# A decoder layer with product-key experts: the order of the v groups, the last u blocks kept on chip, and gathered rows dealt anew

## The chip, the cores and the metric

The kernel runs on one core of a Trainium2 chip. Its time is the device time in microseconds (us) of one execution; a verdict compares the medians of executions of two kernels. The engines are TensorE (PE: matmuls, with PEld for its weight loads), VectorE (DVE), ScalarE (ACT), GpSimd (POOL) and SyncE (SP). ScalarE, GpSimd and SyncE also issue DMA transfers; the sixteen DMA engines of the core carry all of them. Each engine runs its own instructions in the order in which they were written, and waits for others by semaphores.

## The reference

One layer of a hybrid decoder is run for 512 prompt tokens and 64 sample tokens (8 sequences of 8), with width D = 2048. Nearly all of the change lies in its last part, PEER, a layer of 16384 single-neuron experts of which each token uses 8 x 16:

```python
q = (xb @ w_q).reshape(PEER_BLOCK, PEER_HEADS, 2, HALF_DIM)
sc = jnp.einsum('thpk,pnk->thpn', q, sub_keys).astype(jnp.float32)
v1, i1 = lax.top_k(sc[:, :, 0], PEER_TOPK)
v2, i2 = lax.top_k(sc[:, :, 1], PEER_TOPK)
...
g = jax.nn.softmax(top, axis=-1).astype(xb.dtype)
act = jax.nn.gelu(jnp.einsum('td,thkd->thk', xb, expert_u[eidx])) * g
return jnp.einsum('thk,thkd->td', act, expert_v[eidx])
```

An expert's index is i1 * 128 + i2. Before PEER stand a modulated norm, a projection, a gated recurrence and a short convolution with an output projection; after it a residual and the final norm. Everything is in float32.

## The kernel before

**Two ways to the experts.** The kernel ranks the 128 values of i1 by how often they are picked. The experts of the first L = 84 of them (blocks of 128 experts) are computed densely for all 512 prompt tokens on TensorE; picks in the other 44 blocks, and all picks of the 64 samples, are computed sparsely: for each of 128 partitions (a token, or half the picks of a token) one row of `u` or `v` per column of a list is gathered from memory by an indirect DMA from GpSimd, 128 rows of 2048 numbers at once. Such a gather is called a row here. VectorE takes the dot product of a u row with the tokens' `hT` (L1230), or adds a v row, times its weight, to a sum in PSUM (L1258). The rows come in groups: the samples with 64, and five groups of prompt tokens, sorted by how many picks they have left, with 34, 43, 33, 27 and 10 (`GT`). Entries past a token's last pick are out of bounds, and nothing is fetched for them, so the last rows of a group are thin. Each prompt group's u rows begin with one fetch of its tokens (`h2r`, L1211), copied into `hT` by ScalarE (L1217). In all there are NU = 216 u uses (211 rows, 5 copies) and 211 v rows; v goes through the groups in the order 0, 2, 1, 3, 5, 4 (`VO`).

**The u stage.** `NU2` = 168 halves: block i, half c. For each, `load` fetches the block's weights with the SP queue into `raw` (512 KB), ScalarE copies them to `xhi` rounded (L903), GpSimd makes the rest `xlo` (L904), and TensorE runs 24 matmuls (L1356): three products for each of 8 slices, so that float32 accuracy is kept with rounded operands. `ahead(n + 3, n + 2)` loads three halves ahead and splits two ahead. After a block's second half ScalarE applies gelu into a tile `act` (three buffers, L1359) and writes it to memory, `actd` (256 KB, L1360). Beside it the routing weights are built densely block by block and written to memory, `gd`.

**The v stage.** `GROUPS` puts the blocks in ten groups of 8 and one of 4; for each, four quarters q of the output's columns; for each of these, four blocks (SG) at a time. That makes M = 84 steps of four columns kq with 12 matmuls each (L1376). The four blocks of a step share the activations of one such group of four, `sg`. Group sg needs: `load_weights` (four loads of 256 KB from `gd` into `gsb`, one buffer, with 512 contiguous bytes each), `load_group` (1024 KB from `actd` into `actr`, one buffer), `weigh` (their product on VectorE, L1319), and `halve` in two parts, `ahi` on ScalarE (L1326) and `alo` on VectorE (L1330). Both loads are issued on ScalarE's queue. The results in PSUM are moved or added to `acc` (L1396 ScalarE, L1398 VectorE).

**The seam.** For the last 18 halves, from n = E0 = 150 on, the groups sg 0 and 1 (the first eight blocks) are prepared by the code after `u_half`: loads of sg 0 at E0 + 1 to E0 + 4, `weigh` at E0 + 6, `halve` at E0 + 7 and E0 + 8; loads of sg 1 at E0 + 7 to E0 + 10, `weigh` at E0 + 14, `halve` at E0 + 15 and E0 + 16. From sg 2 on, `jobs` holds a list by column, worked out from `hi_at`, the column of the `halve` before it (it starts at -4): for sg 2 loads in columns 0 to 3, `weigh` in 8, `halve` in 12 and 14; the loads of sg 3 begin at column 10.

**The rows' order.** `gather_to(k)` issues uses up to number k, and in front of each use fetches up to three (in v four) rows ahead into four (in v six) slots. In the u stage the rows are dealt first by the time that is left over, and from half R2 on (all rows sorted) evenly, so that EARLY_V = 24 v rows are used by the end; past E0 with 0.8 of the slope. In v they are dealt by `room` (what a column has left) over the costs `cost` of the rows: 1.25 for the samples' rows, 1 for others. The result of a group goes to memory with a scatter, `accd`; groups with 64 tokens need two.

Of the kernel before, what the change touches and what calls it, by code (L numbers as in the profile page):

```python
# [30 lines left out]
NA = NP  # L31
# [19 lines left out]
HEADS_COUNTED = 4  # L51
FULL_ROWS = 1.25
LAG = 3
PAIRS = 6
EARLY_V = 24
HB = 4
# [23 lines left out]
def build(ctx, tc, A, O, dbg=None):  # L80
# [776 lines left out]

    steps, uses_of = [], {}
    b0 = 0
    for gi, sz in enumerate(GROUPS):  # L860
# [18 lines left out]
    def load(n):  # L879
        if n >= len(stream):  # L880
            return
        s = stream[n]
        k = n % 3 if n < NU2 + 2 else (n - NU2 - 2) % 4
        pool, b = (ws, 2) if k < 2 else (wx, 1) if k == 2 else (pools["vx"], 1)
        raw = pool.tile([128, 8, 128], F32, name=f"raw{n}", tag="wraw", bufs=b)
        if s[0] == "U":
            nc.sync.dma_start(raw, A["ut"][bass.ds(block(s[1]), 1), s[2]].rearrange("o p k c -> p (o k) c"))
        else:
            _, i, q = s
            r2 = raw.rearrange("p (a k) c -> p a (k c)", a=2)  # L890
            for a in range(2):
                nc.sync.dma_start(r2[:, a, :], A["vq"][bass.ds(block(i + a), 1), q].rearrange("o p c -> p (o c)"))
        raws[n] = raw
# [410 lines left out]
    def load_group(sg):  # L1304

        acts[sg] = ep.tile([128, SG, NA], F32, name=f"actr{sg}", tag="actr", bufs=1)
        nc.scalar.dma_start(acts[sg], actd[SG * sg:SG * sg + SG].rearrange("i p t -> p i t"))

    def load_weights(sg, q):

        if q == 0:
            gsb[sg] = ep.tile([128, NCH, SG * TC], F32, name=f"gsb{sg}", tag="gsb", bufs=1)
        nc.scalar.dma_start(gsb[sg][:, 4 * q:4 * q + 4, :],
                            gd[4 * q:4 * q + 4, :, sg * SG:(sg + 1) * SG, :].rearrange("c p i t -> p c (i t)"))

    def weigh(sg):

        a = acts[sg].rearrange("p i (c t) -> p i c t", t=TC)
        V.tensor_tensor(a, a, gsb.pop(sg).rearrange("p c (i t) -> p i c t", t=TC), op=ALU.mult)  # L1319

    def halve(sg, part):
# [24 lines left out]
    def u_half(n, i, c):  # L1346
# [10 lines left out]
        if c == 1:  # L1357
            act = actp.tile([128, NA], F32, name=f"act{i}", tag="act")
            S.activation(act, pu, AF.Gelu_apprx_tanh)  # L1359
            nc.scalar.dma_start(actd[i], act)  # L1360

# [236 lines left out]
    for n in range(NU2):  # L1598
# [36 lines left out]
        if not even:  # L1635
            if since is None and ready[0]:
                since = n
            if since is not None and n == since + 1:
                fetch_to(RB - 1)
            if R1 is not None and n > R1 + 1 and gf[0] in h_fetch and gf[0] <= gu[0] + 1:  # L1640
                fetch_to(gf[0] + 1)
# [9 lines left out]
        else:  # L1651
            gather_to(G0 + (NU + EARLY_V - G0) * (n - R2 - 0.2 * max(0, n - E0)) / (0.8 * (NU2 - 1) + 0.2 * E0 - R2))
        if n == E0:
# [5 lines left out]
        u_half(n, i, c)  # L1659
        for sg, o, first in ((0, 1, 0), (1, 8, 1)):  # L1660
            if n - E0 == o + 1:
                load_group(sg)
            if 0 <= n - E0 - o + first < 4:
                load_weights(sg, n - E0 - o + first)
            if n - E0 == o + 5 + sg:
                weigh(sg)
            if n - E0 == o + 6 + sg:
                halve(sg, 0)
            if n - E0 == o + 7 + sg:
                halve(sg, 1)  # L1670
    hp_.close()
# [11 lines left out]
    jobs = {}  # L1683
    hi_at = -4
    for sg in range(2, L // SG):
# [12 lines left out]
    for m in range(last):  # L1698
        for kq in range(KD // VQ):
            room[m, kq] = PIECE / 2 - 0.75 * steps[m][4] - 0.38  # L1700
    tot, run_ = sum(room.values()), 0.0
    fb = finish_b()
    fplan = {(last + 1, 2), (last + 2, 3), (last + 3, 1), (last + 3, 3), (last + 4, 1), (last + 4, 3)}
    NT = len(uses)
    cost = [FULL_ROWS if j < NU + bound[0] else 1.0 for j in range(NV0, NT)]
    sums = [sum(cost[:j + 1]) for j in range(len(cost))]
# [190 lines left out]
```

## Time and profile before

| | before |
|---|---|
| median of 3 runs | 3260.12 us (3255.20 to 3267.94) |
| profiled execution | 3266.23 us, span 3264.3 us |
| PE busy | 3107.0 us (95%) |
| DVE busy | 2144.3 us (66%) |
| POOL busy | 1720.4 us (53%) |
| ACT busy | 1074.1 us (33%) |
| u stage, first to last matmul of L1356 | 1197.6 to 2260.5 us |
| v stage, first to last matmul of L1376 | 2264.8 to 3236.7 us |

A row of a profile names line, engine, operation and tiles (out<-in, buffer numbers left out); "x" is a count. Behind the bar stand the busy time and the mean duration of one in ns, and then the idle time of that engine just before these instructions and who ended it. A row of the timeline begins with the start and the duration in us, and gives in brackets the idle time before it. A wait for several semaphores is put down to the one that came last. "q" behind an engine is its queue of DMA issues; q0, q1 and q10 in the tables of DMA queues are the gathers of GpSimd, the transfers of SP and those of ACT.

### The profile page before, as it was taken

Reading aid. Unit: us, or ns where it says so; the run is one execution under the profiler, and the core shown is the slowest. Engines: PE = TensorE matmul, PEld = TensorE weight load, DVE = VectorE, ACT = ScalarE, POOL = GpSimd, SP = SyncE. Lnnn points to the kernel's source line nnn. Section 1 sums busy time; section 2 is a strip of 40 time slices with the busy share of each in tenths; the row PEclk is TensorE's granted clock in tenths of the full one; section 3 lists DMA queues with packets and bytes.
Section 4 is the critical chain, followed back from the end, with each engine's and each line's share of the span. In section 5 each row is a group of like instructions: output and inputs, shape, how many; then the busy total and the mean of one; then the engine's idle time right before and its main releaser. Section 6 shows DMA issues by size and latency. Waiting matters only on the chain.

```text
span 3264.3 us, 53659 instructions
## 1 busy us (share of the span) xinstructions
PE 3107.0 (95%) x20695; PEld 2634.3 (81%) x20695; DVE 2144.3 (66%) x3238; ACT 1074.1 (33%) x1672; POOL 1720.4 (53%) x985
## 2 busy tenths in 40 slices
PE   5999999999989999999999999997999999999997
PEld 2688889899979998887778888875788888788776
DVE  5455521243346898887988888856566888778745
ACT  3344311132232222222656666522322222222222
POOL 2233233344343336666666666655666777677642
PEclk8999999999989999999999999998999999999998
DMA  9734465523342127889879898998999988899954
GB/s 371 291 137 147 164 217 207 207 82 135 130 155 70 69 89 282 311 309 380 312 288 387 326 382 343 376 355 330 348 349 368 395 315 301 320 376 337 354 183 153
DMA packets 305109, 869.09 MB, mean 266 GB/s; under 512 B 37610, under 2 KB 81514, under 8 KB 256650
## 3 DMA queue, kind: packets, MB, share of 16 engines
q1 hardware_dynamic: 165216, 390.87, 33.1%
q0 software_dynamic: 62880, 386.64, 30.3%
q10 hardware_dynamic: 76752, 88.10, 7.8%
q8 instruction: 163, 2.67, 0.3%
q14 instruction: 98, 0.80, 0.1%
HBM read 865.21 MB, written 68.90 MB: 286 GB/s over the span
## 4 chain that ended last, share of the span: by engine, by line
PE 55%; DMA 8%; issue 3%; DVE 2%; POOL 2%; ACT 0%; SPq 0%; ACTq 0%; POOLq 0%; DVEq 0%
PE pv L1376 23%; PE pu L1356 23%; DMA gsb<-gd 3%; PE qb L138 3%; PE qa L138 3%; DMA raw<-vq 2%; PE gbank L1554 1%; PE gx L1554 1%; DMA u<-u,rows 1%; DMA actd<-act 1%; POOL xlo L904 1%; PE sc L740 0%; PE pv L1380 0%; DMA tok<-accd 0%; DVE acc L1760 0%
## 5 line engine op out<-in xcount | busy, mean ns | idle before, releaser
L904 POOL TENSOR_TENSOR xlo<-raw,xhi 128x1024 fp32r<-128x1024 f32 x336 | 827.5, 2473 | 483.2 <-ACT xhi L903 475.3
L903 ACT ACTIVATE xhi<-raw 128x1024 fp32r<-128x1024 f32 x336 | 355.3, 1061 | 884.4 <-PE pv L1376 406.9
L1230 DVE SCALAR_TENSOR_TENSOR u<-u,hT 128x2048 f32<-128x2048 f32 x211 | 478.1, 2283 | 144.6 <-DMA u<-u,rows 132.8
L1258 DVE SCALAR_TENSOR_TENSOR accB<-v,dots,accB 128x2048 f32<-128x2048 f32 x199 | 468.3, 2353 | 154.5 <-DMA v<-v,rows 151.8
L1356 PE MATMUL pu<-hhi,xhi 128*128 128x512 f32 x1344 | 533.1, 397 | 11.9 <-ACT xhi L903 11.2
L1376 PE MATMUL pv<-ahi,xlo 128*128 128x512 f32 x1344 | 526.5, 392 | 14.2 <-POOL xlo L904 14.2
L1376 PE MATMUL pv<-ahi,xhi 128*128 128x512 f32 x1344 | 528.7, 393 | 11.3 <-ACT acc L1396 7.4
L1356 PE MATMUL pu<-hhi,xlo 128*128 128x512 f32 x1344 | 524.7, 390 | 6.2 <-POOL xlo L904 6.2
L1376 PE MATMUL pv<-alo,xhi 128*128 128x512 f32 x1344 | 526.4, 392 | 0.0
L1356 PE MATMUL pu<-hlo,xhi 128*128 128x512 f32 x1344 | 525.0, 391 | 0.0
L1376 PEld LDWEIGHTS pv<-ahi,xlo 128*128 128x128 f32 x1344 | 254.1, 189 | 71.0 <-POOL xlo L904 18.1
L1356 PEld LDWEIGHTS pu<-hhi,xhi 128*128 128x128 f32 x1344 | 253.2, 188 | 72.1 <-ACT xhi L903 11.6
L1376 PEld LDWEIGHTS pv<-ahi,xhi 128*128 128x128 f32 x1344 | 254.2, 189 | 64.3 <-ACT acc L1396 7.8
L1356 PEld LDWEIGHTS pu<-hhi,xlo 128*128 128x128 f32 x1344 | 253.2, 188 | 61.1 <-POOL xlo L904 8.0
L1376 PEld LDWEIGHTS pv<-alo,xhi 128*128 128x128 f32 x1344 | 254.6, 189 | 52.4
L1356 PEld LDWEIGHTS pu<-hlo,xhi 128*128 128x128 f32 x1344 | 253.3, 188 | 50.1
L1202 POOL DMA_INDIRECT u<-u,rows x211 | 213.3, 1011 | 149.2 <-DVE u L1230 104.4
L1202 POOL DMA_INDIRECT v<-v,rows x211 | 235.7, 1117 | 88.6 <-issue 34.0
L1548 ACT ACTIVATE op<-op,it 128x128 f32<-128x128 f32 x512 | 155.4, 389 | 0.5 <-issue 0.3
L1398 DVE TENSOR_TENSOR acc<-acc,pv 128x512 f32<-128x512 f32 x144 | 96.0, 682 | 86.5 <-PE pv L1376 82.0
L127 POOL TENSOR_TENSOR wlo_q<-raw_q,whi_q 128x1024 fp32r<-128x1024 f32 x28 | 68.0, 2427 | 151.6 <-ACT whi_q L125 151.6
L188 PE MATMUL ada<-wa,cpad 128*32 128x512 f32 x768 | 106.8, 652 | 40.8 <-DMA wa<-w_ada 40.8
(482 smaller groups left out, 5505.2 us busy)
## 6 DMA issues: line engine op xcount, KB each, us to landing
wa<-w_ada SPq DMA_DIRECT2D x96, 1024.0 KB
raw<-ut SPq DMA_DIRECT2D x168, 512.0 KB
raw<-vq SPq DMA_DIRECT2D x336, 256.0 KB
actd<-act ACTq DMA_DIRECT2D x84, 256.0 KB
gd<-stg ACTq DMA_DIRECT2D x64, 336.0 KB
gsb<-gd ACTq DMA_DIRECT2D x84, 256.0 KB
actr<-actd ACTq DMA_DIRECT2D x21, 1024.0 KB
raw_o<-w_out SPq DMA_DIRECT2D x32, 512.0 KB
```

Of the source, the lines that this page charges most:

```text
L127: lo_engine(share).tensor_sub(lo, raw, r32(hi))
L138: PE.matmul(o, st, mv[pick](k), start=first, stop=last)
L188: PE.matmul(acc[32 * g:32 * g + 32, :], cpad[:, 4 * kq + g, :], w[:, g, :], start=kq == 0, stop=kq == 3)
L903: S.activation(hi, raw, AF.Copy)
L904: G.tensor_sub(lo, raw, r32(hi))
L1202: G.indirect_dma_start(out=out, out_offset=None, in_=src, in_offset=bass.IndirectOffsetOnAxis(ap=idx, axis=0), bounds_check=NE * 128 - 1, ...
L1230: V.scalar_tensor_tensor(r, r, 1.0, st["h"], op0=ALU.mult, op1=ALU.mult, accum_out=dots[i][:, j:j + 1])
L1258: V.scalar_tensor_tensor(st["a"], r, dots[i][:, j:j + 1], st["a"], op0=ALU.mult, op1=ALU.add)
L1356: PE.matmul(pu, st[:, kk, :], movA[mv](k), start=k == 0 and a == 0, stop=k == KD - 1 and a == 2)
L1376: PE.matmul(pv, st, mv, start=first and j == 0 and a == 0, stop=last and not end and j == SG - 1 and a == 2)
L1398: V.tensor_add(ak, ak, pv)
L1548: S.activation(ops[:, j0 + j, :], ops[:, j0 + j, :], AF.Copy, scale=it[2][:, b * 4 + j:b * 4 + j + 1])
```

## The change

Six things are changed. (1) The v stage takes the groups of four in another order: first the blocks 0 to 3, then the last four, 80 to 83, then the others (`real`). (2) The gelu results of blocks 80 to 83 are not written to memory and read back: they stay in their `act` tiles, and `weigh_kept` multiplies each by its part of `gsb` straight into `actr`, two in half 166, one in half 167 and the last in column 0 of v; the two parts of `halve` follow in columns 1 and 2. (3) With that `hi_at` starts at 0: for the third group loads in columns 0, 1, 2 and 4, the activations in 5, `weigh` in 12, `halve` in 16 and 18; the weights of the fourth begin at column 14. (4) EARLY_V is 16 in place of 24, and past E0 the rows are dealt with 0.5 of the slope (EASE). (5) In v the room of the first four steps counts 0.7, the samples' rows cost 1, and a row of another group costs 0.35 plus 0.65 times a factor that falls from 1 towards 0 over the last 30% of its group. (6) In the u stage the fetch of a group's tokens may go out when two rows are still to be used, where it was one.

```diff
@@ -49,10 +49,10 @@
 RATE = (1.0, 1.7)
 PIECE_G = 6.3
 HEADS_COUNTED = 4
-FULL_ROWS = 1.25
 LAG = 3
 PAIRS = 6
-EARLY_V = 24
+EARLY_V = 16
+EASE = 0.5
 HB = 4
 SB = 10
 TK = 16
@@ -856,6 +856,12 @@
 
 
     steps, uses_of = [], {}
+    first_sg = [0, L // SG - 1]
+    real_sg = first_sg + [g for g in range(L // SG) if g not in first_sg]
+
+    def real(i):
+        return SG * real_sg[i // SG] + i % SG
+
     b0 = 0
     for gi, sz in enumerate(GROUPS):
         for q in range(VQ):
@@ -889,7 +895,7 @@
             _, i, q = s
             r2 = raw.rearrange("p (a k) c -> p a (k c)", a=2)
             for a in range(2):
-                nc.sync.dma_start(r2[:, a, :], A["vq"][bass.ds(block(i + a), 1), q].rearrange("o p c -> p (o c)"))
+                nc.sync.dma_start(r2[:, a, :], A["vq"][bass.ds(block(real(i) + a), 1), q].rearrange("o p c -> p (o c)"))
         raws[n] = raw
 
     def conv(n):
@@ -1304,19 +1310,30 @@
     def load_group(sg):
 
         acts[sg] = ep.tile([128, SG, NA], F32, name=f"actr{sg}", tag="actr", bufs=1)
-        nc.scalar.dma_start(acts[sg], actd[SG * sg:SG * sg + SG].rearrange("i p t -> p i t"))
+        nc.scalar.dma_start(acts[sg], actd[real(SG * sg):real(SG * sg) + SG].rearrange("i p t -> p i t"))
 
     def load_weights(sg, q):
 
         if q == 0:
             gsb[sg] = ep.tile([128, NCH, SG * TC], F32, name=f"gsb{sg}", tag="gsb", bufs=1)
         nc.scalar.dma_start(gsb[sg][:, 4 * q:4 * q + 4, :],
-                            gd[4 * q:4 * q + 4, :, sg * SG:(sg + 1) * SG, :].rearrange("c p i t -> p c (i t)"))
+                            gd[4 * q:4 * q + 4, :, real(SG * sg):real(SG * sg) + SG, :].rearrange("c p i t -> p c (i t)"))
 
     def weigh(sg):
 
         a = acts[sg].rearrange("p i (c t) -> p i c t", t=TC)
         V.tensor_tensor(a, a, gsb.pop(sg).rearrange("p c (i t) -> p i c t", t=TC), op=ALU.mult)
+
+    kept = []
+
+    def weigh_kept(j):
+
+        if j == 0:
+            acts[1] = ep.tile([128, SG, NA], F32, name="actr1", tag="actr", bufs=1)
+        g = gsb[1] if j < SG - 1 else gsb.pop(1)
+        V.tensor_tensor(acts[1][:, j, :].rearrange("p (c t) -> p c t", t=TC),
+                        kept.pop(0).rearrange("p (c t) -> p c t", t=TC),
+                        g[:, :, j * TC:(j + 1) * TC], op=ALU.mult)
 
     def halve(sg, part):
 
@@ -1357,7 +1374,10 @@
         if c == 1:
             act = actp.tile([128, NA], F32, name=f"act{i}", tag="act")
             S.activation(act, pu, AF.Gelu_apprx_tanh)
-            nc.scalar.dma_start(actd[i], act)
+            if i < L - SG:
+                nc.scalar.dma_start(actd[i], act)
+            else:
+                kept.append(act)
 
     pvs = {}
 
@@ -1637,7 +1657,7 @@
                 since = n
             if since is not None and n == since + 1:
                 fetch_to(RB - 1)
-            if R1 is not None and n > R1 + 1 and gf[0] in h_fetch and gf[0] <= gu[0] + 1:
+            if R1 is not None and n > R1 + 1 and gf[0] in h_fetch and gf[0] <= gu[0] + 2:
                 fetch_to(gf[0] + 1)
             if since is not None and n > since + 2:
                 due_g += RATE[R1 is not None] + (0.7 if waits and spare > 4.5 else 0.0)
@@ -1649,7 +1669,7 @@
                 spare = min(spare, 3.0)
             G0 = gu[0]
         else:
-            gather_to(G0 + (NU + EARLY_V - G0) * (n - R2 - 0.2 * max(0, n - E0)) / (0.8 * (NU2 - 1) + 0.2 * E0 - R2))
+            gather_to(G0 + (NU + EARLY_V - G0) * (n - R2 - (1 - EASE) * max(0, n - E0)) / (EASE * (NU2 - 1) + (1 - EASE) * E0 - R2))
         if n == E0:
             assert not pair and not stg
             put(len(puts))
@@ -1657,17 +1677,22 @@
             epx = ctx.enter_context(ExitStack())
             ep = epx.enter_context(tc.tile_pool(name="ep", bufs=1))
         u_half(n, i, c)
-        for sg, o, first in ((0, 1, 0), (1, 8, 1)):
-            if n - E0 == o + 1:
-                load_group(sg)
-            if 0 <= n - E0 - o + first < 4:
-                load_weights(sg, n - E0 - o + first)
-            if n - E0 == o + 5 + sg:
-                weigh(sg)
-            if n - E0 == o + 6 + sg:
-                halve(sg, 0)
-            if n - E0 == o + 7 + sg:
-                halve(sg, 1)
+        if n - E0 == 2:
+            load_group(0)
+        for sg, o in ((0, 1), (1, 7)):
+            if 0 <= n - E0 - o < 4:
+                load_weights(sg, n - E0 - o)
+        if n - E0 == 6:
+            weigh(0)
+        if n - E0 == 7:
+            halve(0, 0)
+        if n - E0 == 8:
+            halve(0, 1)
+        if n == NU2 - 2:
+            weigh_kept(0)
+            weigh_kept(1)
+        if n == NU2 - 1:
+            weigh_kept(2)
     hp_.close()
     vp = ctx.enter_context(tc.tile_pool(name="vp", bufs=1, side="right"))
     acc = vp.tile([128, KD, NA], F32, name="acc")
@@ -1681,7 +1706,10 @@
     last = M - VQ - ENDS
     KQ = KD // VQ
     jobs = {}
-    hi_at = -4
+    hi_at = 0
+    jobs[0] = [lambda: weigh_kept(3)]
+    jobs[1] = [lambda: halve(1, 0)]
+    jobs[2] = [lambda: halve(1, 1)]
     for sg in range(2, L // SG):
         use = uses_of[sg * SG]
         free = KQ * (uses_of[(sg - 3) * SG][-1] + 1) if sg >= 3 else 0
@@ -1697,12 +1725,16 @@
     room = {}
     for m in range(last):
         for kq in range(KD // VQ):
-            room[m, kq] = PIECE / 2 - 0.75 * steps[m][4] - 0.38
+            room[m, kq] = (PIECE / 2 - 0.75 * steps[m][4] - 0.38) * (0.7 if m < 4 else 1.0)
     tot, run_ = sum(room.values()), 0.0
     fb = finish_b()
     fplan = {(last + 1, 2), (last + 2, 3), (last + 3, 1), (last + 3, 3), (last + 4, 1), (last + 4, 3)}
     NT = len(uses)
-    cost = [FULL_ROWS if j < NU + bound[0] else 1.0 for j in range(NV0, NT)]
+    shares = []
+    for i in VO:
+        c = GT[i][2]
+        shares += [1.0 if not i else 0.35 + 0.65 * min(1.0, (c - j) / (0.3 * c)) for j in range(c)]
+    cost = shares[EARLY_V:]
     sums = [sum(cost[:j + 1]) for j in range(len(cost))]
     for m in range(M):
         gi, q, bl, first, final = steps[m]
```

## The prediction

> **What bounds the kernel now.** I read the busy shares first, then TensorE's own waits around the change from the u stage to the v stage, then, for each wait, the chain of engines behind it, and last the DMA queues in the same stretch.
>
> ```profile
> span 3264.3 us, 53659 instructions
> PE 3107.0 (95%) x20695; PEld 2634.3 (81%) x20695; DVE 2144.3 (66%) x3238; ACT 1074.1 (33%) x1672; POOL 1720.4 (53%) x985
> ...
> L1356 PE MATMUL pu<-hhi,xlo 128*128 128x512 f32 x122 | 48.5, 397 | 2.3 <-POOL xlo L904 2.3
> L1356 PE MATMUL pu<-hhi,xhi 128*128 128x512 f32 x121 | 48.0, 396 | 11.2 <-ACT xhi L903 11.2
> ...
> L1376 PE MATMUL pv<-ahi,xhi 128*128 128x512 f32 x71 | 29.6, 417 | 11.3 <-ACT acc L1396 7.4 <-ACT xhi L903 3.9
> ...
> L1376 PE MATMUL pv<-ahi,xlo 128*128 128x512 f32 x70 | 28.8, 412 | 4.9 <-POOL xlo L904 4.9
> ```
>
> The four matmul rows are for 2162 to 2330 us, the seam. TensorE sets the end (95%), so only its idle time can be won, and 29.7 us of it (2.3 + 11.2 + 11.3 + 4.9) lies in these 168 us. Two stretches of the seam and one of the v stage (columns: length, then busy time of PE, PEld, DVE, ACT, POOL, granted clock, DMA share, GB/s):
>
> ```profile
> 2216.00:2262.00 46.00, 44.75 (x190) 36.65 (x190) 30.54 (x13) 8.16 (x10) 30.77 (x20) 0.97 0.98 384
> ...
> 2316.00:2330.00 14.00, 6.61 (x20) 5.14 (x20) 13.64 (x6) 7.64 (x9) 9.22 (x5) 0.63 0.75 249
> ...
> 2500.00:2640.00 140.00, 140.00 (x619) 115.95 (x618) 107.68 (x65) 31.98 (x28) 100.80 (x60) 1.00 1.02 384
> ```
>
> 619 matmuls in 140 us are 0.226 us each: a v step (48) is 10.9 us, a column of it (12) 2.7 us, a u half (24) 5.4 us. In that v stretch TensorE is never idle, with the DMA engines full. After the seam's waits the granted clock is down (0.97, 0.63), which costs a little more than the idle time.
>
> The first seam wait, from TensorE back:
>
> ```profile
> 2213.70 0.79 PE L1356 MATMUL pu<-hhi,xhi 128*128 128x512 f32 x1 [11.20 <-ACT xhi L903]
> ...
> 2210.80 1.91 ACT L1326 ACTIVATE ahi<-actr 128x2048 fp32r<-128x2048 f32 x1 [18.68 <-DVE actr L1319]
> ...
> 2212.61 1.99 ACT L903 ACTIVATE xhi<-raw 128x1024 fp32r<-128x1024 f32 x2
> ...
> 2208.47 2.29 DVE L1319 TENSOR_TENSOR actr<-actr,gsb 128x2048 f32<-128x2048 f32 x1 [11.68 <-DMA actd<-act]
> ```
>
> `weigh(0)` (L1319) waits for its loads, `halve` (L1326) on ScalarE waits for it, and the next weight split (L903) stands behind `halve` in ScalarE's order. Why the loads are late is in the queues (packets, MB, share): first 2165 to 2175 us, then 2175 to 2208.
>
> ```profile
> q10 hardware_dynamic: 1941, 1.94, 61.0%
> q0 software_dynamic: 119, 0.85, 20.3%
> ...
> q0 software_dynamic: 1281, 9.31, 68.7%
> ...
> q10 hardware_dynamic: 1156, 0.99, 8.9%
> ```
>
> q0 carries the gathered rows, q10 ScalarE's transfers. While rows are few, q10 moves 1.94 MB in 10 us; while they come one on the other (9.31 MB), it moves half of that in 33 us. The load that `weigh` needs crawls behind the rows.
>
> **The change, part by part.** The sum is made against the profiled execution, 3266.23 us, which is 6.1 above the median of the runs (3260.12).
>
> *Thinner rows.* Of the rows fetched before the seam's end, eight go later, and the rest are spread by EASE: past E0 a half uses 0.92 row, where it used 1.44. That is the code's formula, with the switch to even dealing near half 127 and some 174 rows used by then, both an estimate from the order of fetches on GpSimd: 0.5 x (232 - 174) / 31.5 against 0.8 x (240 - 174) / 36.6. The rows fetched between 2158 and 2260 us are:
>
> ```profile
> L1202 POOL DMA_INDIRECT v<-v,rows x22 | 23.8, 1082 | 14.5 <-PE pu L1356 5.9 <-DVE accB L1258 4.2 <-DMA v<-v,rows 2.2
> ...
> raw<-vq SPq DMA_DIRECT2D x51, 256.0 KB
> actr<-actd ACTq DMA_DIRECT2D x4, 1024.0 KB
> ...
> q0 software_dynamic: 4834, 33.22, 58.9%
> ...
> v<-v,rows POOLq DMA_INDIRECT x34
> ```
>
> The last four (2500 to 2640 us) give 0.98 MB for a row, so some 8 MB leave the seam. Keeping four `act` on chip takes away a group's load (1024 KB) and its four writes, 2 MB more. Between 2175 and 2208 us lie six halves: 5.5 rows, 5.4 MB, in place of 9.31. What q10 lacked is under 1 MB, so I put its landing at 2188 to 2198 us. TensorE wants the split at 2213.70 - 11.20 = 2202.5; less 2.29, 1.91, 1.06 and the hand-overs, the load must land by 2197. I take the wait as gone: 11.20 + 1.22 (the second part of it, on `xlo`), and 3% of 46 us for the clock: **-14**; bounds 0 and -15.
>
> *The kept group at the seam.* The arithmetic is the same: four products of a quarter's width for one of 2.29 us; they hide behind the last u half and the first v column. What moves is order. Now:
>
> ```profile
> 2264.80 0.79 PE L1376 MATMUL pv<-ahi,xhi 128*128 128x512 f32 x1 [3.91 <-ACT xhi L903]
> ...
> 2284.99 0.50 PE L1376 MATMUL pv<-ahi,xlo 128*128 128x512 f32 x1 [1.66 <-POOL xlo L904]
> ...
> 2261.47 0.33 ACTq L1360 DMA_DIRECT2D actd<-act  x1
> 2261.90 1.91 ACT L1326 ACTIVATE ahi<-actr 128x2048 fp32r<-128x2048 f32 x1 [11.24 <-DMA actd<-act]
> 2263.71 1.04 ACT L903 ACTIVATE xhi<-raw 128x1024 fp32r<-128x1024 f32 x1
> ...
> 2281.43 1.06 ACT L903 ACTIVATE xhi<-raw 128x1024 fp32r<-128x1024 f32 x1 [5.72 <-DMA raw<-vq]
> ...
> 2267.62 2.28 DVE L1330 TENSOR_TENSOR alo<-actr,ahi 128x2048 fp32r<-128x2048 f32 x1
> ```
>
> u ends at 2260.9 (2264.80 - 3.91), and the first v split reuses the buffer of the last u split, so it can't be sooner. The write and `ahi` in front of it go: 2.6 us won. But `halve(1)` now stands behind the splits of the second step, the last of which ran at 2281.43. Moved 2.6 earlier it ends at 2279.9; `ahi` 1.9 and `alo` 2.3 then bring the second step's second matmul to 2284.3, where now the third starts at 2284.99. Queued behind `ahi` on ScalarE are the loads of the third group and the evacuations of the second step; TensorE waits for both. With lighter queues the raw blocks land up to 3 us sooner. I take **-2**; bounds -5, and +7 if ScalarE's issue of the next `gsb` load in front of `ahi` is held as long as this one:
>
> ```profile
> 2181.27 6.79 ACTq L1360 DMA_DIRECT2D actd<-act  x1
> ```
>
> *The third group's times.* The third wait has the same shape:
>
> ```profile
> 2323.50 0.80 PE L1376 MATMUL pv<-ahi,xhi 128*128 128x512 f32 x1 [7.39 <-ACT acc L1396]
> ...
> 2316.29 2.29 DVE L1319 TENSOR_TENSOR actr<-actr,gsb 128x2048 f32<-128x2048 f32 x1 [15.90 <-DMA gsb<-gd]
> ...
> 2318.61 0.37 ACTq L1313 DMA_DIRECT2D gsb<-gd  x1
> ```
>
> `weigh(2)` is late, so ScalarE is held at the load of group 3 (one buffer) from column 10, the evacuations of columns 12 to 15 stand behind it, and TensorE stops at column 16. With `hi_at` 0 `weigh(2)` is due at column 12 and that load at 14, so TensorE would notice at 18; and rows come at 1.5 a step there (factor 0.7), not 2. I take it as gone: 7.39 and the clock (6.61 busy at 0.63, 2.4): **-9.5**; bounds 0 and -10. From then on each group's `halve` stands one column later than now, the second part five columns (13.6 us) ahead of its use: nothing, the cover is those columns against its 2.3 us, and without them that is the price.
>
> *The earlier h2 row* (`gu + 2`). It matters where the second group of u rows begins:
>
> ```profile
> 1714.07 1.35 PE L1554 MATMUL gbank<-wr,op 128*32 128x84 f32 x32 [7.72 <-ACT stg L1561]
> ...
> 1711.49 1.88 ACT L1217 ACTIVATE hT<-h2r 128x2048 f32<-128x2048 f32 x1 [7.60 <-DMA h2r<-h2d,tok]
> ...
> 1705.47 0.95 POOL L1211 DMA_INDIRECT h2r<-h2d,tok  x1 [0.30 <-issue]
> ...
> 1705.02 2.29 DVE L1230 SCALAR_TENSOR_TENSOR u<-u,hT 128x2048 f32<-128x2048 f32 x1 [0.16 <-DMA u<-u,rows]
> ```
>
> The fetch goes out a half earlier and lands (6.0 us, 1705.47 to 1711.49) in time; then the last dot that reads the old `hT` binds, 1707.3. **-4**; bounds 0 and -7.7. The other boundaries wait for sorted rows or are dealt evenly: nothing.
>
> *Eight more rows in v, dealt by shares.*
>
> ```profile
> L1202 POOL DMA_INDIRECT v<-v,rows x177 | 198.0, 1119 | 69.2 <-issue 30.4 <-DMA accd<-v,tok 14.4 <-DMA gsb<-gd 11.4
> ...
> L1258 DVE SCALAR_TENSOR_TENSOR accB<-v,dots,accB 128x2048 f32<-128x2048 f32 x169 | 397.6, 2353 | 115.1 <-DMA v<-v,rows 112.7
> ...
> L1376 PE MATMUL pv<-ahi,xlo 128*128 128x512 f32 x1121 | 437.6, 390 | 9.4 <-POOL xlo L904 9.4
> ```
>
> Eight rows are 19 us of VectorE (8 x 2.353), 9 of GpSimd, 8 MB. The cover is TensorE's v work: VectorE alone sits idle 115 us before rows there. Counted from the code, full rows come at 2.5 a step from step 4 on, where now it is 2 at first and 2.6 from the second group on; at 2.6 (2500 to 2640 us) TensorE was busy 140.00 of 140. So nothing; uncovered the 8 MB at 384 GB/s would be +20. In the thin tails up to 6 rows fall in one step: 6 x 2.353 = 14.1 of VectorE against 10.9, a lag of 3, within a step's lead: 0 to +15 over five groups. The 9.4 us behind the scatters to `accd` stay (0 to twice that). Together **+2**.
>
> On the other hand, the page "DMA: Bandwidth & Descriptors" of the Trainium skill, section "Specifications", gives a core about 358 GB/s from HBM. By it a step's 4.0 MB (2.5 rows, 1.05 of `vq`, 0.5 of weights and activations), 369 GB/s, would not fit, some 30 steps would stretch by 3%, and the sum, an estimate, would be 10 us higher. The 384 GB/s above contradict it, and the measurement decides.
>
> **Sum:** -14 - 2 - 9.5 - 4 + 2 = -27.5; 3266.2 - 27.5 - 6.1 = **3233**.
>
> **The rivals.**
> - *The first wait stays*: the loads still land after 2197, since q10 only gets leavings until the rows in flight are through. For it: the estimate's late end, 2198. Then -13.5: 3247.
> - *A new wait takes its place*: `ahi` of the kept group is held by the issue in front of it (+7), and the evacuations behind it keep the third wait (0): -14 + 7 - 4 + 2 = -9: 3251. For it: 6.79 us above. Against: the queue is lighter.
> - *Slower: the crawl comes into every group of v.* Denser full rows from step 4 on hold each `gsb` load past its `weigh`, ScalarE stops at the next group's load, and each four steps lose what was lost at 2323.50, 10 us. Groups 3 to 8, until the rows thin: +60 - 27.5: 3293. From the third such wait on it is slower than now, from the fifth by over 0.5%. Against: 2.6 rows a step without one.
> - *The late waits go as well* (-9.4): 3223.
>
> **How the numbers follow.** Forecast 0.58 (own range 3218 to 3244), first wait stays 0.14, new wait 0.11, slower 0.12, late waits go 0.05. The range goes from all gains at their bounds with the late waits gone (-15 - 5 - 10 - 7.7 - 9.4: 3213) to 3264, past the second and third case, and leaves out the fourth and a little. A measurement tells 0.5%, 16 us, from no change: faster is below 3244. That is nearly all of the forecast and of the fifth case, a third of the second and a little of the third: 0.66; slower is the fourth case, 0.12; between them 0.22.
>
> **What would show it.** Right: no idle before a `pu` matmul near 2213 and none at the fifth v step; `weigh(0)` idle under 2 us; the `hT` copy at half 84 waiting some 3 us; PE idle from step 4 to 2820 still 0. Wrong: TensorE waiting over 5 us for `ahi` or `alo` in the second v step; ScalarE held at a `gsb` issue in v; `pv` waiting for `xlo` more than 10 us in all; or gaps of the same length elsewhere, the rows' bytes being late where they went.

## The result, and the profile after

The changed kernel takes **3242.76 us** (median of 7 runs, 3237.66 to 3256.85) where the one before takes 3260.94 (7 runs): a ratio of **0.9947, 95% interval 0.9925 to 0.9969**. The forecast was 3233, its range 3213 to 3264. It is faster by about the 0.5% that was put down as what can be told from no change; the interval lies wholly below 1. The profiled execution took 3244.53 us, against 3266.23.

The head of the page after, and below it TensorE's groups over the same 168 us at the seam as in the prediction (instructions, then busy us and mean ns of one, then the idle time before them and what ended it):

```profile
span 3242.5 us, 53658 instructions
PE 3110.3 (96%) x20695; PEld 2635.4 (81%) x20695; DVE 2151.4 (66%) x3241; ACT 1072.8 (33%) x1672; POOL 1731.1 (53%) x985
```

```profile
L1373 PE MATMUL pu<-hhi,xlo 128*128 128x512 f32 x120 | 46.8, 390 | 0.5 <-POOL xlo L910 0.5
L1373 PE MATMUL pu<-hhi,xhi 128*128 128x512 f32 x119 | 46.3, 389 | 0.0
L1396 PE MATMUL pv<-ahi,xhi 128*128 128x512 f32 x111 | 44.8, 404 | 1.0 <-ACT xhi L909 1.0
L1396 PE MATMUL pv<-ahi,xlo 128*128 128x512 f32 x110 | 44.7, 406 | 3.3 <-POOL xlo L910 3.3
L1396 PE MATMUL pv<-alo,xhi 128*128 128x512 f32 x110 | 44.5, 404 | 1.9 <-DVE alo L1347 1.9
```

Of 29.7 us of idle time 6.7 are left (0.5 + 1.0 + 3.3 + 1.9), the last of them new: `pv` waits for the kept group's `alo`. The two waits of 11.20 and 7.39 us are gone. Three of the prediction's stretches, moved about as far as the work moved (columns as there):

```profile
2200.00:2246.00 46.00, 44.61 (x196) 36.31 (x194) 25.17 (x13) 10.80 (x13) 24.40 (x15) 1.00 0.75 284
2295.00:2309.00 14.00, 14.00 (x64) 11.58 (x63) 8.59 (x3) 5.79 (x6) 8.17 (x4) 1.00 0.73 233
2480.00:2620.00 140.00, 138.02 (x607) 113.52 (x606) 107.70 (x65) 33.02 (x30) 105.15 (x60) 1.00 1.00 379
```

The granted clock came back with the waits (1.00 where 0.97 and 0.63 stood). But in the v stretch TensorE is no longer busy all the time. There the late waits on `xlo` made room for others (2470 to 3100 us, before and after):

```profile
L1376 PE MATMUL pv<-ahi,xlo 128*128 128x512 f32 x908 | 354.7, 391 | 9.4 <-POOL xlo L904 9.4
```

```profile
L1396 PE MATMUL pv<-ahi,xhi 128*128 128x512 f32 x898 | 352.3, 392 | 12.5 <-DVE acc L1418 7.4 <-DVE dots L1259 4.0 <-ACT xhi L909 1.0
L1396 PE MATMUL pv<-ahi,xlo 128*128 128x512 f32 x899 | 351.3, 391 | 0.0
```

TensorE now idles 12.5 us there in place of 9.4. Of these, 11.4 end with VectorE: 7.4 when it has emptied a PSUM bank into `acc`, and 4.0 that the profile puts down to the short instruction (`dots`) right behind such an addition. In a second profile of the same kernel (e10 below) the sum is 9.4, the same as before the change.

### The profile page after: what moved, and what is told of

Same layout as the page of the kernel before. It is cut to its first block, busy times and chain, and to the rows that moved or that the text cites. A ratio compares the mean times of both kernels' runs of the same rounds, so it can differ in the third digit from the quotient of the medians.

```text
span 3242.5 us, 53658 instructions
## 1 busy us (share of the span) xinstructions
PE 3110.3 (96%) x20695; PEld 2635.4 (81%) x20695; DVE 2151.4 (66%) x3241; ACT 1072.8 (33%) x1672; POOL 1731.1 (53%) x985
## 4 chain that ended last, share of the span: by engine, by line
PE 53%; DMA 7%; issue 4%; DVE 3%; POOL 2%; ACT 0%; SPq 0%; POOLq 0%; DVEq 0%; ACTq 0%
PE pu L1373 24%; PE pv L1396 20%; PE qb L138 3%; PE qa L138 3%; DMA actr<-actd 2%; DMA v<-v,rows 1%; POOL xlo L910 1%; PE gbank L1574 1%; DMA gsb<-gd 1%; DVE accB L1264 1%; PE gx L1574 1%; POOL u L1208 1%; DMA raw<-vq 1%; PE sc L740 0%; DVE alo L1347 0%
## 5 line engine op out<-in xcount | busy, mean ns | idle before, releaser
L1208 POOL DMA_INDIRECT v<-v,rows x211 | 248.8, 1179 | 85.5 <-issue 35.9
L127 POOL TENSOR_TENSOR wlo_o<-raw_o,whi_o 128x1024 fp32r<-128x1024 f32 x32 | 77.7, 2428 | 115.8 <-ACT whi_o L125 111.6
```

What stands on the lines that cost most here:

```text
L127: lo_engine(share).tensor_sub(lo, raw, r32(hi))
L1208: G.indirect_dma_start(out=out, out_offset=None, in_=src, in_offset=bass.IndirectOffsetOnAxis(ap=idx, axis=0), bounds_check=NE * 128 - 1, ...
```

## The experiments

Each kernel's stretches are taken from the starts of TensorE's matmuls (24 in a half, 48 in a step) in its one profiled execution: from half 150 to the first v matmul (the first wait), from there to step 3 (the transition), steps 3 and 4 (the third wait), and from step 20 to the last v matmul. The ratios, with their 95% intervals, are to the kernel before, run beside it; they are near the quotients of the medians, not the same.

| kernel | first wait | transition | third wait | late v | ratio |
|---|---|---|---|---|---|
| before | 118.4 | 40.3 | 31.7 | 736.7 | 1 |
| changed | 99.8 | 42.8 | 21.8 | 741.5 | 0.9947 |
| e1 rows of before | 115.8 | 42.7 | 21.8 | 733.5 | 0.9959 (0.9943 to 0.9976) |
| e2 before + rows | 100.8 | 38.9 | 33.5 | 766.2 | 1.0037 (1.0023 to 1.0051) |
| e3 old times | 105.3 | 44.6 | 21.8 | 735.9 | 0.9950 (0.9932 to 0.9969) |
| e4 no thin start | 99.6 | 44.1 | 21.8 | 739.1 | 0.9924 (0.9897 to 0.9952) |
| e5 both old | 100.8 | 42.6 | 21.8 | 738.5 | one run, 3244.30 us |
| e6 not kept | 106.8 | 38.9 | 21.8 | 735.2 | 0.9904 (0.9876 to 0.9933) |
| e7 flat shares | 100.4 | 42.7 | 21.8 | 746.1 | 0.9960 (0.9931 to 0.9989) |
| e8 kept in two | 100.5 | 39.4 | 21.8 | 735.1 | 0.9904 (0.9881 to 0.9928) |
| e9 old deal | 103.3 | 44.5 | 21.8 | 757.1 | 1.0000 (0.9982 to 1.0017) |
| e10 changed, again | 100.8 | 45.3 | 21.8 | 735.9 | 0.9939 (0.9922 to 0.9956) |
| e11 kept in two, again | 100.0 | 39.3 | 21.8 | 737.2 | 0.9918 (0.9895 to 0.9940) |
| e12 in two, eased | 100.9 | 39.5 | 21.8 | 737.9 | 0.9944 (0.9923 to 0.9966) |

**Which part took the first wait away?** e1 puts the rows of before back into the changed kernel; e2 puts the new rows alone into the kernel before.

```diff
-EARLY_V = 16          # e1, in the changed kernel
-EASE = 0.5
+EARLY_V = 24
+EASE = 0.8
```

> The changed kernel with the row dealing of before up to the seam (EARLY_V 24, EASE 0.8); the kept group, the third group's times and the shares in v stay. My theory, that the rows' bytes hold the first gsb load: the idle before a pu matmul near half 160 comes back, 8 to 14 us of it, the stretch from half 150 to the first v matmul is 110 to 116 us where the changed kernel has 99.8 and the one before 118.4, and the time is 3250 to 3258. Rival, that the 2 MB less of the kept group freed the load: the stretch stays within 3 us of 99.8, and with eight fewer rows in v the time is 3238 to 3243.

```diff
-EARLY_V = 24          # e2, in the kernel before
+EARLY_V = 16
-    ... (n - R2 - 0.2 * max(0, n - E0)) / (0.8 * (NU2 - 1) + 0.2 * E0 - R2)
+    ... (n - R2 - 0.5 * max(0, n - E0)) / (0.5 * (NU2 - 1) + 0.5 * E0 - R2)
```

> The kernel before with only the row dealing changed (EARLY_V 16, EASE 0.5). My theory: the first wait goes by this alone, the stretch from half 150 to the first v matmul falls from 118.4 to 101 to 106 us (the waits at the seam that belong to the second group stay), and the third wait at the fifth v step stays, so that the third and fourth steps and the fifth's start (m3 to m5) still take 29 to 32 us; time 3245 to 3250. Rival, both parts needed: at least 6 us of idle stay before a pu matmul near half 160, and the time is 3252 to 3258.

e1's wait in the timeline of TensorE, then e2's groups at the seam:

```profile
2213.21 0.79 PE L1373 MATMUL pu<-hhi,xhi 128*128 128x512 f32 x1 [11.39 <-ACT xhi L909]
```

```profile
L1356 PE MATMUL pu<-hhi,xhi 128*128 128x512 f32 x119 | 46.3, 389 | 0.0
L1376 PE MATMUL pv<-ahi,xhi 128*128 128x512 f32 x98 | 39.9, 407 | 10.2 <-ACT acc L1396 9.2 <-ACT xhi L903 1.0
```

With the old rows the wait is back, 11.39 us where it was 11.20, kept group or not; with the new rows alone it is gone, and the third wait stays (9.2; the stretch, 33.5, is above the 29 to 32 expected). So the rows, and not the 2 MB of the kept group, held `weigh(0)`; the rival fell. Which of the two did it, the eight rows that leave or the thinner spacing of the others, was not tried. What I had not expected is e2's time: slower than before, since late v grew by 29.5 us. The rows that leave the seam cost more there than both waits, until they are dealt otherwise.

**Which part took the third wait away?** e3 and e4 each undo one part in the changed kernel, e5 both; e6 keeps both and undoes the kept group and the group order.

```diff
-    hi_at = 0                                       # e3 and e5
+    hi_at = -4
-    room[m, kq] = (...) * (0.7 if m < 4 else 1.0)    # e4 and e5
+    room[m, kq] = (...)
```

> The changed kernel with the due times of before for the third and later groups (hi_at -4); the thin start of the rows in v (factor 0.7) stays. My theory, that the times took the third wait away: weigh(2) is due four columns sooner than its loads land, ScalarE is held at the load of group 3, and the stretch from step 3 to step 5 goes from 21.8 to 27 to 31 us; time 3248 to 3252. Rival, that the thin start and the lighter queue let the loads land in time: 21.8 to 24 us, time within 3 us of the changed kernel.

> The changed kernel without the factor 0.7 for the rows of the first four v steps. My theory, that the times carry the third wait: steps 3 to 5 stay at 21.8 to 24 us, and the time stays within 3 us. Rival, that the thin start carries it: 27 to 31 us there, time 3248 to 3252.

> The changed kernel with the due times of before (hi_at -4) and without the factor 0.7, the kept group staying: with one of the two undone the third wait stayed away (21.8 us from step 3 to step 5 both times; weigh(2) ran 40.5 us after the first v matmul with the factor alone, due from column 8, and 49.3 us after it with the later times alone, due from column 12, against 51.5 us in the kernel before). Theory, that each covers for the other: with both undone weigh(2) runs 46 to 50 us after the first v matmul and steps 3 to 5 take 26 to 31 us. Rival, that the kept group alone took the wait away, its loads of group 2 being issued earlier: 21.8 to 24 us.

e6 is the kernel before with EARLY_V, EASE, `hi_at` = 0, the factor 0.7, the shares and `gu + 2` of the changed one.

> The changed kernel with the group order, the kept group and its step order undone (all eleven groups through the chip's memory as before); row dealing, shares, times, factor 0.7 and the earlier h2 row as changed. Theory, that the kept group only moves order at the seam and its four products and late halve cost TensorE 3 to 5 us in the first three v steps: the stretch from the first v matmul to step 3 is 38 to 40 us (changed kernel 42.8), steps 3 to 5 stay at 21.8 to 24 us by the times, and the time is 3236 to 3243 where the changed kernel has 3243. Rival, that the kept group is what lets the loads of group 2 land: steps 3 to 5 take 27 to 32 us, and the time is 3248 to 3254.

The wait stayed away in all four: my theory held in e4 and e6, and fell in e3 and e5, where the rival's stretch came. (e3's median, 3251.83 us, lies where my theory had it, but the kernel before took 3266.72 beside it, and the ratio is that of the changed kernel.) `weigh(2)` in the timeline of VectorE, first in e5, where the kept group stands alone, then in e2, which has none of the three:

```profile
2292.57 2.29 DVE L1325 TENSOR_TENSOR actr<-actr,gsb 128x2048 f32<-128x2048 f32 x1 [7.92 <-DMA gsb<-gd]
```

```profile
2297.93 2.29 DVE L1319 TENSOR_TENSOR actr<-actr,gsb 128x2048 f32<-128x2048 f32 x1 [14.78 <-DMA gsb<-gd]
```

It runs 44.6 us after the first v matmul (2247.9) in e5 and 52 us after it (2246.0) in e2. So the times with the thin start are enough without the kept group (e6), and the kept group is enough without them (e5). The new rows and shares were there both times; the wait also stays away without the rows (e1) and without the shares (e9), with all three parts in place. Without the kept group the transition takes 38.9 us in place of 42.8, though e6's profile also shows a part of the first wait (106.8). The times or the thin start alone, without the kept group, were not run.

**What do eight more rows cost in v?** e7 deals all rows alike; e9 takes the costs of before.

```diff
-    shares += [1.0 if not i else 0.35 + 0.65 * min(1.0, (c - j) / (0.3 * c)) for j in range(c)]
+    shares += [1.0 if not i else 1.0 for j in range(c)]                    # e7
...
-    cost = shares[EARLY_V:]
+    cost = [1.25 if j < NU + bound[0] else 1.0 for j in range(NV0, NT)]    # e9
```

> The changed kernel with all rows of the v stage dealt alike (shares 1.0, no thinner tails). The kernel before with the changed row dealing up to the seam alone lost some 28 us after v step 20 against the kernel before. Theory, that eight more rows don't fit under TensorE when dealt evenly, and the shares are what hides them: from step 20 to the last v matmul the changed kernel's 741.5 us become 755 to 775 us, with TensorE idle behind VectorE's adds, and the time is 3255 to 3272. Rival, that the loss there came from the later groups' times (hi_at -4) and the eight rows fit either way: 738 to 748 us, time within 5 us of the changed kernel.

> The changed kernel with the row costs of before in the v stage (1.25 for the rows of the first list, 1.0 for all others). From step 20 to the last v matmul the changed kernel took 741.5 us, the kernel before with only the row dealing changed 766.2, and the changed kernel with flat shares 745.9. Theory, that the 1.25 is what made the eight rows dear, since it leaves more rows to the later steps (28 in ten steps, where the flat shares have 27 and the kernel before 26): 758 to 770 us. Rival, that the later groups' old times did it: 742 to 750 us.

e7's theory fell (746.1), its rival too in its reason: e9 shows the 1.25 at work, 757.1, just below the 758 to 770 expected, and with it the whole gain is gone (1.0000). e9's groups from 2470 to 3100 us, and after them one such place in the timelines of GpSimd, VectorE and TensorE (start, length, in brackets the idle time ahead):

```profile
L1396 PE MATMUL pv<-ahi,xhi 128*128 128x512 f32 x878 | 345.6, 394 | 21.0 <-DVE acc L1418 21.0
```

```profile
2859.31 1.02 POOL L1208 DMA_INDIRECT v<-v,rows  x1 [6.53 <-DMA accd<-v,tok]
...
2868.00 2.36 DVE L1264 SCALAR_TENSOR_TENSOR accB<-v,dots,accB 128x2048 f32<-128x2048 f32 x1 [9.26 <-DMA v<-v,rows]
2870.26 1.28 DVE L1418 TENSOR_TENSOR acc<-acc,pv 128x512 f32<-128x512 f32 x2
...
2871.09 0.77 PE L1396 MATMUL pv<-ahi,xhi 128*128 128x512 f32 x1 [6.04 <-DVE acc L1418]
```

GpSimd stands behind a scatter, the rows behind it are fetched late, VectorE waits for a row with the addition to `acc` queued behind it, and TensorE waits for that. It is the longest such place. After step 20 TensorE waits 20.7 us for VectorE in waits of over 0.3 us: 13.5 us stand behind rows that VectorE waited for, as here, and 7.2 behind an instruction of VectorE that took far longer than its usual time (the last section has these). Three stretches of e9, the first with the DMA engines full, the others not:

```profile
2480.00:2620.00 140.00, 139.86 (x617) 115.36 (x615) 113.21 (x65) 32.56 (x30) 101.36 (x60) 1.00 1.01 385
2620.00:2760.00 140.00, 132.72 (x577) 107.77 (x578) 113.64 (x68) 30.77 (x28) 99.67 (x59) 1.00 0.87 308
2760.00:2900.00 140.00, 130.56 (x560) 106.53 (x559) 109.32 (x63) 30.87 (x28) 101.64 (x60) 0.98 0.91 336
```

VectorE is busy 109 to 114 us of 140 in all three, so its work is not the limit; and TensorE is idle for 0.14 us where 385 GB/s are moved and for 7 to 9 where 308 and 336 are, so the bytes are not either. What is left is the order: which late rows and slow instructions stand in front of which additions to `acc`. That is argued from these rows, and no run changed the order alone. Of e2's 29.5 us the 1.25 explains 11.0 (757.1 - 746.1) and the flat shares up to 8.9 (746.1 less the median 737.2 of the changed dealing); the other 9.6 remain open. All this is from one execution each, and the nine with the changed dealing range from 735.1 to 741.5.

**A better transition.** e8 (and e11, the same again) splits the kept group's halving: the first two blocks at the last u half, the last two at the first columns.

```diff
         if n == NU2 - 1:
+            halve_kept(0, 0)       # ahi of blocks 0 and 1
+            halve_kept(0, 1)       # alo of blocks 0 and 1
             weigh_kept(2)
...
-    jobs[1] = [lambda: halve(1, 0)]
-    jobs[2] = [lambda: halve(1, 1)]
+    jobs[1] = [lambda: halve_kept(2, 0)]
+    jobs[2] = [lambda: halve_kept(2, 1)]
```

> The changed kernel with halve(1) done in two: the first two blocks of the kept group are split at the last u half, the last two at the first v columns; TensorE's matmuls and the bytes stay. Theory, that TensorE's idle in the second v step (1.9 us behind alo in the changed kernel, 1.8 and 2.3 us in a run of it with other times) is the whole splitting standing behind two weight splits: that idle goes, and the stretch from the first v matmul to step 3 falls from 42.8 to 39 to 41 us; time 2 to 4 us less. Rival, that what is late there are the weight splits themselves, the v blocks not having landed: the idle only moves to the split weights and the stretch stays at 42 to 45 us.

> The changed kernel itself, for a time on the same chip as the two versions below: 0.993 to 0.996 of the kernel before. Its stretches show how much the same program moves from one execution to the next: 99 to 107 us from half 150 to the first v matmul, 42 to 45 us from there to step 3.

> The version that splits the kept group in two, against the changed kernel on the same chip. Theory, that 3 to 4 us of the transition are won: 0.990 to 0.993 of the kernel before, and 0.1% less than the changed kernel. Rival, that the difference seen so far was between chips: the same ratio as the changed kernel within 0.05%.

e12 is e8 with `EASE = 0.35`.

> The version that splits the kept group in two, with rows thinner still past E0 (EASE 0.35): some 10 rows leave the last 17 halves for the halves ahead of them. Theory, that the first seam wait was left at its edge (in two runs it came back by 5 to 7 us, with weigh(0) waiting 9 us): weigh(0) waits under 2 us, the stretch from half 150 to the first v matmul is 99 to 101 us, and the time is the split version's or up to 3 us less. Rival, that the rows moved ahead hold TensorE or the loads there: that stretch or the ones from half 90 to half 150 (398 us) grow by 3 us or more.

e8's groups at the seam:

```profile
L1408 PE MATMUL pv<-ahi,xlo 128*128 128x512 f32 x111 | 44.1, 397 | 4.5 <-POOL xlo L910 4.5
L1408 PE MATMUL pv<-alo,xhi 128*128 128x512 f32 x111 | 43.7, 394 | 0.0
```

The wait for `alo` is gone and the transition takes 39.4 and 39.3 us, against 42.8 and 45.3. On one chip e11 ran 3236.06 us (median of 6), the changed kernel 3242.53 (12), the one before 3266.90 (25); the ratios are 0.9918 against 0.9939. Their intervals overlap, but all six times of e11 (up to 3237.50) lie below eleven of the twelve of the changed kernel (from 3241.20). The stretches do not overlap: 39.3 to 39.5 in the three executions with the group in two, 42.6 to 45.3 in the eight that keep it whole. e6 does as well without keeping anything (0.9904). e12 is slower than e11 (3245.69 us, median of 8), and its rival holds: a wait in u is longer than in the others,

```profile
2116.77 1.35 PE L1586 MATMUL gbank<-wr,op 128*32 128x84 f32 x32 [7.63 <-ACT stg L1593]
```

and half 90 to half 150 took 403.8 us, where the changed kernel has 398.0 and e8 and e11 400.3 and 397.8, with 4.0 and 2.9 us of idle time there. `weigh(0)` still waited 4 us, so its theory fell there too.

## Why the prediction was right, and where it was not

From half 150 to step 5 it forecast -14 - 2 - 9.5 = -25.5; the profiles show 190.4 to 164.4 us, **-26.0** (e10, the same kernel, has 167.9: -22.5). The earlier h2 row was to give -4 and gave -1.0 in this pair; v from step 5 on was to cost 2 and cost 5.6 (0.8 up to step 20, 4.8 after); the rest gave 0.3. That is -21.7 in place of -27.5. The other 4 us are the offset: I took the 6.1 us by which the profile of before lay above its median for both kernels, and the changed kernel's lies 1.8 above its own.

- **Thinner rows: right, mechanism and size.** In the first stretch they are worth 16.0 us (e1 against the changed kernel) and 17.6 (before against e2), where 14 was forecast. The rows fetched from 2158 us to the end of u (14 where there had been 22), the queues from 2173 to 2206 us (packets, MB, share; in the kernel before it was 2175 to 2208), and `weigh(0)` in the timeline:

```profile
L1208 POOL DMA_INDIRECT v<-v,rows x14 | 17.7, 1266 | 2.1 <-issue 0.9 <-DVE accB L1264 0.3 <-PE pu L1373 0.2
```

```profile
q0 software_dynamic: 863, 6.29, 48.8%
...
q10 hardware_dynamic: 2814, 2.06, 19.3%
```

```profile
2185.60 3.60 DVE L1325 TENSOR_TENSOR actr<-actr,gsb 128x2048 f32<-128x2048 f32 x1 [0.90 <-DMA gsb<-gd]
```

In 33 us there are 6.29 MB of rows (5.4 were estimated) and 2.06 MB of loads, in place of 9.31 and 0.99. The load landed at 2185.6, ahead of the 2188 to 2198 that I gave it. The rival with the late end has its place all the same: in e3 and e6 `weigh(0)` ran at 2194.5 and 2199.9, and the stretch was 5.5 and 7 us longer.

- **The kept group: the step that failed is the 2.6 us won.** With the old rows it is won (e1: 118.4 to 115.8). With the new ones the group's loads land early in any case, and the wait at the first v matmul falls from 3.91 to 1.0 without a kept group too (e2). The price that I saw, `halve(1)` behind the splits of the second step, was larger than the 0.6 that I gave it; from the timelines of ScalarE, VectorE and TensorE:

```profile
2258.61 1.06 ACT L909 ACTIVATE xhi<-raw 128x1024 fp32r<-128x1024 f32 x1 [3.54 <-DMA raw<-vq]
2259.57 1.90 ACT L1343 ACTIVATE ahi<-actr 128x2048 fp32r<-128x2048 f32 x1
...
2261.50 2.80 DVE L1347 TENSOR_TENSOR alo<-actr,ahi 128x2048 fp32r<-128x2048 f32 x1 [4.58 <-ACT ahi L1343]
...
2264.36 0.50 PE L1396 MATMUL pv<-alo,xhi 128*128 128x512 f32 x1 [1.90 <-DVE alo L1347]
```

  The chain is the one described. Against the 38.9 us without the kept group (e2, e6) the transition is 3.9 us longer here and 6.4 in e10; against the kernel before, 2.6 and 5.0. The column in which this wait falls takes 6.5 us where e8 has 2.7: 1.9 are idle, and the rest is slower matmuls (the granted clock over the transition is 0.88, in e8 0.96). The 2.0 us more that the first stretch gave (18.6 for 14 + 2.6) make up for it by luck, in the sum and not in the reason.

- **The third wait: right size (-9.9), but not for the reason given alone.** I gave it to the times; either they with the thin start (e6) or the kept group (e5) removes it, by landing `weigh(2)` before the load of group 3 stops ScalarE for TensorE.

- **The earlier h2 row: the term was mis-sized at the landing.** I took 6.0 us for it; it took 10.7. A row of u had gone out 4.1 us ahead of it (1694.88), where before the last one had gone 11.4 us ahead; that this is the cause was not tried by itself. From the timelines of GpSimd, ScalarE and TensorE:

```profile
1694.88 1.00 POOL L1208 DMA_INDIRECT u<-u,rows  x1 [2.95 <-DVE u L1236]
...
1698.98 0.97 POOL L1217 DMA_INDIRECT h2r<-h2d,tok  x1 [0.65 <-DVE u L1236]
...
1709.71 1.88 ACT L1223 ACTIVATE hT<-h2r 128x2048 f32<-128x2048 f32 x1 [6.93 <-DMA h2r<-h2d,tok]
...
1712.30 1.35 PE L1574 MATMUL gbank<-wr,op 128*32 128x84 f32 x32 [7.06 <-ACT stg L1581]
```

  The fetch goes out 6.5 us earlier than in the kernel before and lands 1.8 earlier. The copy waits 6.93 us, not 3, and TensorE 7.06 where it had 7.72. Over all executions, half 80 to half 90 is 74.4 us (median of twelve with the change) against 76.2 and 77.6 (two without): some -2.5. But two of the twelve, e6 and e7, take 77.0, so the size is uncertain.

- **Eight more rows in v: +2 was near, the step beneath it wrong.** In the nine executions with 16 early rows and the shares late v is 735.1 to 741.5, median 737.2, against 736.7: next to nothing, as forecast. But that is a sum of two parts: e1, with the shares and 24 early rows, has 733.5 in its one execution, so the eight rows cost some 3.7 and the shares win about as much. I took the cover to be TensorE's v work as such, and its loss to be bytes. e2 and e9 show 29 and 20 us for the same rows under the old costs: the shares are the cover. The lag that I gave to the thin tails came in size (11.4 us behind VectorE), but mostly not from them: 6.7 us stand behind instructions of VectorE that took far longer than usual (the last section), and 4.0 behind the last row of a group, which landed late. My sign that TensorE would not idle from step 4 to 2820 us failed: it idled 8.2 us. The late scatter waits did go, against "these stay"; the one took the place of the other.

The page "DMA: Bandwidth & Descriptors" of the Trainium skill, section "Specifications", would have had the v steps stretch by its 358 GB/s. No run bears that out; e10 moves 390 GB/s with TensorE always busy:

```profile
2340.00:2480.00 140.00, 140.00 (x619) 115.91 (x619) 106.89 (x63) 37.23 (x35) 104.50 (x60) 1.00 1.03 390
```

Of the rivals, the slower one did not come as a time, though its sign did. After 2310 us the changed kernel runs `weigh` 18 times; 15 times a `gsb` issue follows within 0.1 us of its end, with ScalarE idle for 2 to 16 us ahead of it. In the kernel before it is 16 of 19, the third wait among them. So ScalarE is held at that issue in nearly every group, before and after. What failed is the rival's next step: from 2320 us on TensorE waits for `xhi` once, 1.0 us. In e4 the wait came through once, 6.13 us (timelines of VectorE, ScalarE and TensorE):

```profile
2822.36 2.29 DVE L1325 TENSOR_TENSOR actr<-actr,gsb 128x2048 f32<-128x2048 f32 x1 [11.05 <-DMA actr<-actd]
...
2824.69 0.37 ACTq L1319 DMA_DIRECT2D gsb<-gd  x1
2825.23 1.06 ACT L909 ACTIVATE xhi<-raw 128x1024 fp32r<-128x1024 f32 x1 [20.05 <-DVE actr L1325]
...
2830.05 0.77 PE L1396 MATMUL pv<-ahi,xhi 128*128 128x512 f32 x1 [6.13 <-ACT xhi L909]
```

## What to carry to other kernels

Work moved out of a stretch has to be priced where it lands by the way it is dealt there: the same eight rows cost some 4 us or 29. When several edits are each said to remove one wait, undo them one by one and then together; here two of them were enough each by itself, and one of these cost 4 to 6 us elsewhere. And a transfer that goes out earlier need not take as long as it did in its old place: its landing is to be estimated from a row with the neighbours that it will have.

## What the runs showed that I had not expected

The subtraction `alo` (128 x 2048) takes 2.28 us, or up to three times that. Its rows (xcount, then ns min/median/max) before, after, and in e5:

```profile
L1330 DVE TENSOR_TENSOR alo<-actr,ahi x21: 2282/2285/4449, 2217.7 to 3118.0; 128x2048 fp32r<-128x2048 f32 x21
```

```profile
L1347 DVE TENSOR_TENSOR alo<-actr,ahi x21: 2283/3135/6243, 2198.2 to 3100.2; 128x2048 fp32r<-128x2048 f32 x21
```

```profile
L1347 DVE TENSOR_TENSOR alo<-actr,ahi x21: 2281/2285/6893, 2200.6 to 3098.3; 128x2048 fp32r<-128x2048 f32 x21
```

In the changed kernel 18 of the 21 lie over a weight split on GpSimd (by more than 0.3 us), as in e10; before 8, in e3 and e5 10. None of the others took over 2.29 us. Two places in the timelines of GpSimd, VectorE and TensorE:

```profile
2476.05 4.78 POOL L910 TENSOR_TENSOR xlo<-raw,xhi 128x1024 fp32r<-128x1024 f32 x2
...
2478.00 4.98 DVE L1347 TENSOR_TENSOR alo<-actr,ahi 128x2048 fp32r<-128x2048 f32 x1
2482.91 0.67 DVE L1418 TENSOR_TENSOR acc<-acc,pv 128x512 f32<-128x512 f32 x1
...
2483.63 0.50 PE L1396 MATMUL pv<-ahi,xhi 128*128 128x512 f32 x1 [1.92 <-DVE acc L1418]
...
2945.38 4.76 POOL L910 TENSOR_TENSOR xlo<-raw,xhi 128x1024 fp32r<-128x1024 f32 x2
...
2945.17 5.00 DVE L1259 TENSOR_TENSOR dots<-dots,gwt 128x10 f32<-128x10 f32 x1
...
2953.20 0.50 PE L1396 MATMUL pv<-ahi,xhi 128*128 128x512 f32 x1 [2.72 <-DVE acc L1418]
```

`alo` ends at 2482.98, 2.15 after the splits end at 2480.83, nearly its own 2.28: it seems to have stood still until they were through. The small product `dots` takes 0.2 us for the other groups of tokens; here it takes 5.00 and ends with the splits. So the due times, one column later, set nearly each `halve` under GpSimd's splits, which I had put at nothing. The page "SBUF — State Buffer" of the Trainium skill, section "SBUF: two separate sides", says that a VectorE instruction with two SBUF inputs and a GpSimd instruction that reads SBUF exclude each other from a shared pair of ports: the one that starts first holds it for its whole instruction, and the other is blocked. The rows agree as far as VectorE's side goes.

In late v of the changed kernel TensorE waits four times for an addition to `acc` that stands behind such an instruction: 1.92, 1.16 and 0.94 us behind `alo` and 2.72 behind `dots`, 6.7 us in all. The kernel before has no such wait there. But e5, with the old times and fewer such meetings, has three behind `alo`, 6.6 us in all, so the number of meetings alone does not set the cost. What it adds to the whole stretch is not settled: e3 and e5, with the old times, have late v at 735.9 and 738.5, within the spread of the others.

One program's stretches also move between executions by several us: the transition took 42.8 and 45.3 in the changed kernel and e10, which are the same program. The first stretch took 99.6 to 106.8 over all kernels with the new rows at the seam.
